# Modulation multiplies gated by weight chunks with tiles loaded two ahead, x_c loaded through ScalarE's queue, and two more raw buffers for the feed-forward output

## The chip, the core and the metric

The kernel runs on one core of a Trainium2 chip. The core's engines work side by side, each through its own instructions in a fixed order: PE (TensorE, matmuls; PEld is its weight load), DVE (VectorE), ACT (ScalarE), POOL (GpSimd) and SP (SyncE, which here only issues DMAs). ACT and POOL issue DMAs too. The metric is the device time of one execution in microseconds (us). Three runs of the kernel before gave 1420.67, 1426.11 and 1424.01, a median of 1424.01.

## What is computed

Two layers over 256 latent and 256 context tokens of width 1024, all in float32. Layer 0 mixes tokens with a bidirectional mLSTM, layer 1 with latent attention; a gated feed-forward with a short convolution follows each. Around every sub-layer stands an adaptive normalization, whose scales, shifts and gates come from a conditioning vector:

```python
m = jax.nn.silu(cond) @ w + b                 # six vectors of 1024 a layer ("modulation")
h = x * (1 + scale) + shift
x = layer_norm(ALPHA * x + gate * sublayer(h))
```

There are two conditionings, c for latent and c_ctx for context tokens. The modulation is a product of a vector with a 1024 x 6144 matrix in each layer. This case is about where that product is done.

## The kernel before

Each float32 matmul is made of three (`mm3`, lines 375 to 377): a weight and an activation are each split into a rounded high part, cast by ACT (L315 for weights, L380 for activations), and a low remainder, subtracted by DVE (L318, L381); then high x high, high x low and low x high are accumulated.

**The weight stream** (`Stream`). Weights come in chunks of 128 x 1024 floats, 512 KB, in one order fixed by `_plan`. SP loads a chunk into a raw buffer (L273), ACT and DVE split it into one of three `w` buffers (NB = 3), PE multiplies. So at most two chunks are split ahead of the one in use. There are three raw buffers of their own; some stages borrow others, as the rings in `Stream.__init__` say: during w_v also `acc`, `ar` and `u` tiles (11 in all), from `("fout0", 0, 0)` the two `acc`, from `("aout", 0, 0)` the three `ar`. A borrowed buffer is free only when its last user has read it.

**The stages**, with the time PE spends on one chunk: a start-up with the first five `up` chunks; `w_up` (5.46 us), which also evacuates x_m and x_c (a convolution of x_m) to DRAM through POOL; `w_og` (5.46), with the background generator `x_sums`, which reads x_m back; `w_v` (2.73), two halves p = 0 and 1 that multiply sums of blocks; `gates`; four heads of `w_qk` (8 chunks of 5.46 each) with the attention of the head before in the background; the output projection `mout`, context then latent (2.73); LayerNorm; feed-forward 0 (`ffn_pre`, `ffn_in`, then `fout0` at 2.73); and layer 1.

**Background work.** `bg` and `bg2` are Python generators; `tick(n, n2)` after a chunk takes n steps of the first and adds n2 to an account that buys steps of the second. This places instructions in the program. Outside the start-up, where the order is written out by hand, the tile library then orders each engine's instructions at build time: of those whose inputs are there by its own estimate, the one earliest in the program comes first. So an instruction without a data dependency can be pulled far ahead of its place. The order is fixed when the kernel runs: an instruction that waits holds all behind it on its engine.

**The modulation in the background** (`bg2`). For each of the vectors (layer l, index c), `ada_bg` takes eight tiles of 128 x 1024 of the transposed matrix. For each tile and condition, one DVE multiply (L506, 128 x 1024) with `bc[j]`, the SiLU of the condition broadcast to all partitions, leaves the sum of its products in one column. There are 80 tiles and 128 multiplies: two a tile for c = 2 to 5 of layer 0 and c = 0, 1 of layer 1, one a tile for the rest. A generator step is one multiply. Vectors 0 and 1 of layer 0 are made in the start-up by PE. The vector (0, 2), a gate, goes with `w_og`; the other nine go with the query-key heads, `mout` and `ffn_in`. A gate's columns are transposed and written to DRAM (L513 to L516).

**The pace.** The tiles of the matrix lie in three `ar` buffers. So that the order does not pull their loads far ahead, `pace` (L518) makes each load wait for the stream: ACT copies one element of the last used weight chunk to `tok` (L521), POOL copies it into the tile (L522), and only then may SP's DMA (L501) write the tile. `bc` is loaded in the same way (L531) and passes through SiLU (L532).

**x_c.** `xc_load` (L682) reads x_c back from DRAM through POOL's queue and splits it. It is called from the second half of `w_v`, after 6 of its first 16 chunks and 10 of its last 12; nothing else holds these loads but a free `s2` buffer.

Of the kernel before, what the change touches and what calls it, by code (L numbers as in the profile page):

```python
# [7 lines left out]
F32 = mybir.dt.float32  # L8
# [20 lines left out]
NEG = -1e30  # L29
CW = 1024  # L30

NB, NRAW, NU, NAR, NS = 3, 3, 31, 3, 15

SUMS = 5

# [3 lines left out]

VE = {1: (3, 0), 2: (3, 0), 3: (3, 0)}  # L40

ADA_T, ADA_Q, ADA_M, ADA_F = 1.25, 1.5, 0.5, 1.2

# [10 lines left out]
TAIL = {"mout": 4, "fout0": 6, "aout": 7, "fout1": 6}  # L54
# [174 lines left out]
class Stream:  # L229


    def __init__(self, k, ids, order, ws):
        self.k, self.ids, self.order, self.ws = k, ids, order, ws
        self.n = len(order)
        self.nl = self.ns = self.nu = 0
        self.live, self.kept = [], []
        self.limit = self.n
        self.raw, self.hl, self.tags = {}, {}, {}
        self.nsum = 0

        keys = [x[0] for x in order]
        self.bufs = [(0, [("raw", NRAW)] * NRAW)]
        self.bufs.append((keys.index(("vt2", 0, 0)), [("acc", 2)] * 2 + [("ar", NAR)] * NAR + [("u", NU)] * 3 + self.bufs[0][1]))
        self.bufs.append((keys.index(("gates", 0, 0)), self.bufs[0][1]))
        self.bufs.append((keys.index(("fout0", 0, 0)), self.bufs[-1][1] + [("acc", 2)] * 2))
        self.bufs.append((keys.index(("aout", 0, 0)), self.bufs[-1][1] + [("ar", NAR)] * NAR))

    def ring(self, j):
        return [x for x in self.bufs if x[0] <= j][-1]
# [97 lines left out]
class K:  # L347
# [141 lines left out]
    def ada_bg(self, l, c, nconds):  # L489


        nc = self.nc
        if c in (2, 5):
            v = self.adav
            col = v[:, 0:8 * nconds].rearrange("p (j k) -> p k j", k=8)
        else:
            col = self.modc[l, c][:, :, 0:nconds]
        for k in range(8):
            w = self.pool.tile([128, 1024], F32, tag="ar", name="ar", bufs=NAR)
            self.pace(w)  # L500
            nc.sync.dma_start(w, self.a["adaT"][l, c, k])  # L501
            for j in range(nconds):
                if j:
                    yield
                o = self.pool.tile([128, 1024], F32, tag="junk", name="junk", bufs=1) if j + 1 < nconds else w
                nc.vector.scalar_tensor_tensor(o, w, 1.0, self.bc[j], op0=ALU.mult, op1=ALU.mult,  # L506
                                               accum_out=col[:, k, j:j + 1])
            yield
        b = self.smc("ada_c")[:, 48 * l + 8 * c:48 * l + 8 * c + 8].unsqueeze(2).to_broadcast([128, 8, nconds])
        nc.vector.scalar_tensor_tensor(col, col, 1.0 if c in (1, 4) else 0.0, b, op0=ALU.add, op1=ALU.add)  # L510
        if c in (2, 5):
            t = self.pool.tile([128, 32], F32, tag="adat", name="adat", bufs=1)
            nc.vector.transpose(t, v)  # L513
            for q in range(4):
                nc.sync.dma_start(self.gd[l, c].rearrange("j (k q i) -> q (j k) i", q=4, i=32)[q, 0:8 * nconds],
                                  t[32 * q:32 * q + 8 * nconds])  # L516

    def pace(self, t):  # L518

        k = self.pool.tile([1, 1], F32, tag="tok", name="tok", bufs=6)  # L520
        self.nc.scalar.copy(k, self.st.last[0:1, 0:1].bitcast(F32))  # L521
        self.nc.gpsimd.tensor_copy(t[0:1, 0:1], k)  # L522

    def ada_all(self, items):

        nc = self.nc
        self.bc = []
        for j in range(2):
            r = self.pool.tile([128, 1024], F32, tag="acc", name="bc", bufs=2)
            self.pace(r)  # L530
            nc.sync.dma_start(r, self.a["crow"][j:j + 1, :].to_broadcast([128, 1024]))  # L531
            nc.scalar.activation(r, r, AF.Silu)  # L532
            self.bc.append(r)
        for l, c in items:
            yield from self.ada_bg(l, c, 2 if l == 0 or c < 2 else 1)
        self.bc = None
# [25 lines left out]
    def start_up(self):  # L562

        nc, st = self.nc, self.st
# [5 lines left out]
        w, ps, raws = [], [], []  # L570
        src = self.a["ada_w"][0]
        self.adaw, self.xT = {}, []
        for op, g in LOADS:
            f0, f1 = GROUPS[g] if op != "r" else (0, 0)
            if op == "a":
                wd = 128 * (f1 - f0)
                nk = 512 // wd
                self.adaw[g] = []
                for k in range(8):
                    if k % nk == 0:  # L580
                        t = self.uf("adaw")
                        self.adaw[g].append(t)
                    ap = bass.AP(tensor=src.tensor, offset=src.offset + k * 128 * 6 * D + f0 * 128,
                                 ap=[[6 * D, 128], [D, 2], [1, wd]])
                    c = k % nk * 2 * wd
                    nc.sync.dma_start(t[:, c:c + 2 * wd].rearrange("p (a b) -> p a b", a=2), ap)
            elif op == "x":
                for i in range(f0, f1):
                    x = self.s2("xT")
                    nc.sync.dma_start(x, self.a["tokT"][i])  # L590
                    self.xT.append(x)
            else:
                n, _ = st.ids["up", g, 0]
                r = self.pool.tile([128, 1024], F32, tag="raw" if g < 3 else "ar", name="raw0",
                                   bufs=NRAW if g < 3 else NAR)
                nc.sync.dma_start(r, st.ws[n])
                raws.append(r)

# [73 lines left out]
    def w_up(self):  # L672
        st = self.st
        for m in range(NUP, 16):
            w = st.use(("up", m, 0))
            ps = self.ps("up")
            for k in range(8):
                c = slice(k * 128, (k + 1) * 128)
                self.mm3(ps, (w[0][:, c], w[1][:, c]), (self.hT[k][:, 0], self.hT[k][:, 1]), k == 0, k == 7)
            self.up_evac(m, ps)  # L680

    def xc_load(self, k):  # L682
        x = self.s2("xcr")
        self.nc.gpsimd.dma_start(x, self.xcd[k])
        u = self.u("xc")
        self.split(u[:, 0], u[:, 1], x)
        self.xc.append(u)
# [573 lines left out]
    def ffn_in(self, l, hT, n, nt, pre=()):  # L1261
        nc, st = self.nc, self.st
        cw, cb = self.smc("fcw%d" % l), self.smc("fcb%d" % l)
        key = "fin%d" % l
        acts = []
        pre = list(pre)
        for p in range(NF):
            pss = []
            for j in range(2):
                if pre:  # L1270
                    w, ps = pre.pop(0)
                    self.ffn_half(ps, w, hT, 1)
                    if not pre:
                        st.unhold()
                else:
                    w = st.use((key, p, j))
                    ps = self.ps("fin")
                    for k in range(8):
                        c = slice(k * 128, (k + 1) * 128)
                        hi, lo = hT(k)  # L1280
                        self.mm3(ps[:, :n], (w[0][:, c], w[1][:, c]), (hi, lo), k == 0, k == 7)
                pss.append(ps)
                self.tick(nt, ADA_F)
            tmp = self.s2("fg")
# [110 lines left out]
    def rope_load(self):  # L1395
        self.ropet = []
        for t in range(2):
            r = self.pool.tile([128, 2, 512], F32, tag="ar", name="rope", bufs=NAR)
            self.nc.sync.dma_start(r, self.a["rope"][:, t * 128:(t + 1) * 128, :].rearrange("a p f -> p a f"))
            self.ropet.append((r[:, 0], r[:, 1]))  # L1400

# [173 lines left out]
def build(tc, off, a, out):  # L1575
    es = ExitStack()
    with es:
        k = K(tc, es, off, a)
        nc = k.nc
# [2 lines left out]
        k.setup()  # L1582
        st.skip(NUP)
        k.start_up()
        k.w_up()
        k.bg2.append(k.ada_all(((0, 2),)))
        k.bg = [k.x_sums()]
        k.w_og()
        while k.bg2:
# [23 lines left out]
        hn = lambda i: (k.hn[i][:, 0], k.hn[i][:, 1])  # L1613
# [13 lines left out]
        gate = k.bcast(k.gd[0, 2][1:2, :], "gate")  # L1627
# [17 lines left out]
        pl = k.acc4()  # L1645
        xr = k.res_load(tokr, 2)
        gate = k.bcast(k.gd[0, 2][0:1, :], "gate")
        k.outmm("mout", range(16 - TAIL["mout"]), hn, pl, 256, 16, 1, n2=ADA_M)
        k.drain()
        k.outmm("mout", range(16 - TAIL["mout"], 16), hn, pl, 256, 16, 1, True)  # L1650
        k.hn = {}
# [14 lines left out]
        gate = k.bcast(k.gd[0, 5][1:2, :], "gate")  # L1666
# [88 lines left out]
```

## Time and profile before

| what | value |
|---|---|
| median of three runs | 1424.01 us |
| the profiled execution, its own time | 1425.35 us |
| its span, first to last instruction | 1423.6 us |
| mean granted clock of TensorE | 0.989 |
| busy ACT / POOL | 690.2 us (48%) / 159.0 us (11%) |
| moved by DMA | 288.97 MB, mean 203 GB/s |
| modulation tiles, issue to landing | 3.3 / 3.6 / 10.6 us (least, median, most) |
| x_c loads, issue to landing | 5.3 / 6.2 / 14.7 us |

The profile is one execution of the kernel, recorded by the chip. An engine's busy time is the time in which it runs instructions, without DMA issues and semaphores. A wait is idle time of an engine ahead of an instruction, put down to the event that ended it ("PE sc L376 <- DVE qk L381" means that PE stood before a matmul of line 376 into the tile `sc`, until DVE's line 381 had written `qk`; then the total, the number and the longest). A timeline gives start, duration, engine, line, operation, tiles, and in brackets the idle time before. An x with a number counts instructions. The granted clock is the share of full speed that TensorE was given. In 20 us windows it is 1.00 from 0 to 420 and then below 0.98 in six places: 0.74 in 420 to 440, 0.95 and 0.96 in 620 to 660, 0.84 in 720 to 740, 0.91 in 1080 to 1100 and in 1220 to 1240, and at the very end.

PE is idle for 45 us of the span: 9.7 in the first 40 us (start-up), 4.1 from 1400 on, 6 in layer 1 and the rest in the stages from `w_v` to the start of feed-forward 0.

### The profile page before, as it was taken

The page shows a single profiled execution, that of the slowest core. Times are in us where ns is not written, and L with a number is a line of the kernel's source. Part 1 is how long each engine was busy: PE and PEld are TensorE (multiplying, and loading weights), DVE is VectorE, ACT ScalarE, POOL GpSimd, SP SyncE. Part 2 cuts the span into 40 slices and gives each one's busy share as a digit, 9 for nine tenths or more (in the row PEclk, how much of TensorE's full clock was granted, in tenths as well). Part 3 has the DMA queues.
Part 4 walks back from the last instruction along what each step waited for, and adds up shares of the span by engine and source line. Part 5 has one row for each costly group of instructions (what it writes and reads, how often), then busy time and mean ns, then how long its engine had stood idle before and what let it go on. Part 6 is the DMA issues. An engine that isn't in the chain of part 4 may idle for free.

```text
span 1423.6 us, 19222 instructions
## 1 busy us (share of the span) xinstructions
PE 1378.8 (97%) x6969; PEld 1159.0 (81%) x6969; DVE 1032.5 (73%) x1627; ACT 690.2 (48%) x1113; POOL 159.0 (11%) x293
## 2 busy tenths in 40 slices
PE   7999999999998999989989999999999999999997
PEld 3788887777777888878888888888888988899986
DVE  6677856687577687878889776764577888867764
ACT  6576443345433355364644343334364667555551
POOL 0023100112111011102012000120000001000000
PEclk9999999999998999999999999999999999999999
DMA  9477867777654454637647566686665424467660
GB/s 339 160 242 272 324 222 249 253 261 212 217 186 163 133 192 132 213 129 280 223 155 260 191 209 209 219 276 215 193 203 189 140 87 164 148 188 224 211 207 30
DMA packets 90238, 288.97 MB, mean 203 GB/s; under 512 B 11288, under 2 KB 19736, under 8 KB 90144
## 3 DMA queue, kind: packets, MB, share of 16 engines
q1 hardware_dynamic: 69824, 224.29, 46.7%
q0 software_dynamic: 16576, 54.56, 11.9%
q10 hardware_dynamic: 3744, 8.91, 1.6%
q8 instruction: 54, 0.88, 0.3%
q14 instruction: 40, 0.33, 0.1%
HBM read 261.46 MB, written 26.26 MB: 202 GB/s over the span
## 4 chain that ended last, share of the span: by engine, by line
PE 76%; DMA 10%; DVE 6%; issue 4%; ACT 2%; POOL 1%; SPq 0%; DVEq 0%; POOLq 0%; ACTq 0%
PE fin L375 8%; PE fin L377 8%; PE fin L376 8%; PE y L376 5%; PE y L377 5%; PE y L375 5%; DMA raw<-in_ws 4%; PE qk L375 3%; PE qk L376 3%; PE qk L377 3%; PE tok L376 3%; PE tok L377 3%; PE tok L375 3%; DMA ar<-in_adaT 2%; PE up L375 2%
## 5 line engine op out<-in xcount | busy, mean ns | idle before, releaser
L315 ACT CAST w<-raw 128x1024 fp32r<-128x1024 f32 (+2 forms) x289 | 301.5, 1045 | 321.5 <-PE fin L377 81.1
L318 DVE TENSOR_TENSOR w<-raw,w 128x1024 fp32r<-128x1024 f32 (+2 forms) x289 | 350.2, 1214 | 138.9 <-ACT w L315 138.2
L375 PE MATMUL fin<-h,w 128*128 128x256 f32 (+1 forms) x696 | 232.1, 335 | 0.0
L376 PE MATMUL fin<-h,w 128*128 128x256 f32 (+1 forms) x696 | 232.1, 334 | 0.0
L377 PE MATMUL fin<-h,w 128*128 128x256 f32 (+1 forms) x696 | 231.8, 334 | 0.0
L375 PEld LDWEIGHTS fin<-h,w 128*128 128x128 f32 x696 | 132.9, 192 | 12.8
L376 PEld LDWEIGHTS fin<-h,w 128*128 128x128 f32 x696 | 132.8, 191 | 12.9
L377 PEld LDWEIGHTS fin<-h,w 128*128 128x128 f32 x696 | 132.7, 191 | 12.7
L506 DVE SCALAR_TENSOR_TENSOR ar<-ar,bc 128x1024 f32<-128x1024 f32 x80 | 97.8, 1222 | 41.5 <-DMA ar<-in_adaT 35.6
L375 PE MATMUL qk<-xc,w 128*128 128x512 f32 x256 | 100.9, 394 | 0.0
L377 PE MATMUL qk<-xc,w 128*128 128x512 f32 x256 | 99.9, 390 | 0.0
L376 PE MATMUL qk<-xc,w 128*128 128x512 f32 x256 | 99.9, 390 | 0.0
L506 DVE SCALAR_TENSOR_TENSOR junk<-ar,bc 128x1024 f32<-128x1024 f32 x48 | 58.6, 1220 | 53.1 <-DMA ar<-in_adaT 53.1
L522 POOL COPY ar<-tok 1x1 f32<-1x1 f32 x80 | 42.0, 529 | 482.4 <-ACT tok L521 338.8
L375 PE MATMUL y<-w,act 128*128 128x512 f32 (+1 forms) x212 | 80.4, 379 | 0.0
L376 PE MATMUL y<-w,act 128*128 128x512 f32 (+1 forms) x212 | 80.1, 378 | 0.0
L377 PE MATMUL y<-w,act 128*128 128x512 f32 (+1 forms) x212 | 80.1, 378 | 0.0
L375 PEld LDWEIGHTS qk<-xc,w 128*128 128x128 f32 x256 | 48.2, 188 | 10.1 <-issue 0.4
L377 PEld LDWEIGHTS qk<-xc,w 128*128 128x128 f32 x256 | 48.1, 188 | 10.0
L376 PEld LDWEIGHTS qk<-xc,w 128*128 128x128 f32 x256 | 48.2, 188 | 9.7
L652 ACT ACTIVATE fg<-fg 128x512 f32<-128x512 f32 (+1 forms) x44 | 23.0, 523 | 68.0 <-DVE fg L650 68.0
L318 DVE TENSOR_TENSOR wu<-raw,wu 128x1024 fp32r<-128x1024 f32 x36 | 43.4, 1221 | 10.5 <-ACT wu L315 9.8
(399 smaller groups left out, 3043.2 us busy)
## 6 DMA issues: line engine op xcount, KB each, us to landing
raw<-in_ws SPq DMA_DIRECT2D x306, 512.0 KB, 4.3
ar<-in_adaT SPq DMA_DIRECT2D x80, 512.0 KB, 3.6
adaw<-in_ada_w SPq DMA_DIRECT2D x32, 256.0 KB, 6.0
xmd<-xr POOLq DMA_DIRECT2D x16, 256.0 KB, 2.9
xcd<-cv POOLq DMA_DIRECT2D x16, 256.0 KB, 2.8
xs<-xmd POOLq DMA_DIRECT2D x16, 256.0 KB, 4.5
od<-o ACTq DMA_DIRECT2D x16, 256.0 KB, 6.1
t2d<-raw ACTq DMA_DIRECT2D x8, 512.0 KB, 3.9
```

Source lines behind the costliest of these rows:

```text
L315: k.nc.scalar.copy(h[:, :cols], src)
L318: k.nc.vector.tensor_sub(l[:, :cols], src, h[:, :cols])
L375: mm(out, w[0], x[0], start=start, stop=False)
L376: mm(out, w[0], x[1], start=False, stop=False)
L377: mm(out, w[1], x[0], start=False, stop=stop)
L506: nc.vector.scalar_tensor_tensor(o, w, 1.0, self.bc[j], op0=ALU.mult, op1=ALU.mult, accum_out=col[:, k, j:j + 1])
L522: self.nc.gpsimd.tensor_copy(t[0:1, 0:1], k)
L652: nc.scalar.activation(tmp[:, :n], tmp[:, :n], AF.Silu)
```

## The change

- **The pace is replaced by a gate.** `pace` is gone. `gate` is one ACT copy of an element of the last used weight chunk, and it goes into the column where the multiply will leave its sum (partition 0). The multiply, not the load, must now wait for that chunk. POOL takes no part.
- **Tiles are loaded two ahead.** `ar_load` takes the next tile of a list; two are loaded when `ada_all` starts, and the first step of each tile loads one more before its multiplies. The three buffers are now tags `ar` (2) and `ar1` (1) in turn.
- **Steps.** A step is one multiply, as before. New are three steps of prologue: after the `bc` loads come two ends of a step, then the SiLU, then one more. The product now goes to `junk` for both conditions.
- **Where the steps go.** (0, 2) starts with `w_up`, one step a chunk, and goes on in `w_og` with 0.8 (1.25 before). The others: 1.6 steps a chunk in the heads (1.5 before), 0.6 in `mout` (0.5), 1.3 in `ffn_in` (1.2) but none at p = 0; and none in the latent `mout` after its sixth chunk (12 before).
- **x_c** is loaded through ACT's queue, each load behind a gate on its own tile.
- **Raw buffers.** `fout0` borrows the two `acc`, `ar1` and `junk`, four instead of two, but from its ninth chunk on; from `aout` on two `ar` are added, nine in all instead of eight.

```diff
-NB, NRAW, NU, NAR, NS = 3, 3, 31, 3, 15
+NB, NRAW, NU, NS = 3, 3, 31, 15
-ADA_T, ADA_Q, ADA_M, ADA_F = 1.25, 1.5, 0.5, 1.2
+ADA_U, ADA_T, ADA_Q, ADA_M, ADA_F = 1, 0.8, 1.6, 0.6, 1.3
@@ Stream.__init__
-        self.bufs.append((keys.index(("vt2", 0, 0)), [("acc", 2)] * 2 + [("ar", NAR)] * NAR + [("u", NU)] * 3 + self.bufs[0][1]))
+        self.bufs.append((keys.index(("vt2", 0, 0)), [("acc", 2)] * 2 + [("ar", 2), ("ar", 2), ("ar1", 1)] + [("u", NU)] * 3 + self.bufs[0][1]))
         self.bufs.append((keys.index(("gates", 0, 0)), self.bufs[0][1]))
-        self.bufs.append((keys.index(("fout0", 0, 0)), self.bufs[-1][1] + [("acc", 2)] * 2))
-        self.bufs.append((keys.index(("aout", 0, 0)), self.bufs[-1][1] + [("ar", NAR)] * NAR))
+        self.bufs.append((keys.index(("fout0", 0, 8)), self.bufs[-1][1] + [("acc", 2)] * 2 + [("ar1", 1), ("junk", 1)]))
+        self.bufs.append((keys.index(("aout", 0, 0)), self.bufs[-1][1] + [("ar", 2)] * 2))
@@ ada_bg
         for k in range(8):
-            w = self.pool.tile([128, 1024], F32, tag="ar", name="ar", bufs=NAR)
-            self.pace(w)
-            nc.sync.dma_start(w, self.a["adaT"][l, c, k])
+            w = self.art.pop(0)
+            self.ar_load()
             for j in range(nconds):
-                if j:
-                    yield
-                o = self.pool.tile([128, 1024], F32, tag="junk", name="junk", bufs=1) if j + 1 < nconds else w
+                o = self.pool.tile([128, 1024], F32, tag="junk", name="junk", bufs=1)
+                self.gate(col[0:1, k, j:j + 1])
                 nc.vector.scalar_tensor_tensor(o, w, 1.0, self.bc[j], op0=ALU.mult, op1=ALU.mult,
                                                accum_out=col[:, k, j:j + 1])
-            yield
+                yield
@@
-    def pace(self, t):
-
-        k = self.pool.tile([1, 1], F32, tag="tok", name="tok", bufs=6)
-        self.nc.scalar.copy(k, self.st.last[0:1, 0:1].bitcast(F32))
-        self.nc.gpsimd.tensor_copy(t[0:1, 0:1], k)
+    def gate(self, ap):
+
+        self.nc.scalar.copy(ap, self.st.last[0:1, 0:1].bitcast(F32))
+
+    def ar_load(self):
+
+        if self.arq:
+            l, c, k = self.arq.pop(0)
+            w = self.pool.tile([128, 1024], F32, tag=("ar", "ar", "ar1")[self.nar % 3], name="ar", bufs=(2, 2, 1)[self.nar % 3])
+            self.nar += 1
+            self.nc.sync.dma_start(w, self.a["adaT"][l, c, k])
+            self.art.append(w)
@@ ada_all
-            self.pace(r)
+            self.gate(r[0:1, 0:1])
             nc.sync.dma_start(r, self.a["crow"][j:j + 1, :].to_broadcast([128, 1024]))
+            self.bc.append(r)
+        self.arq = [(l, c, k) for l, c in items for k in range(8)]
+        self.art, self.nar = [], 0
+        for _ in range(2):
+            self.ar_load()
+        for _ in range(2):
+            yield
+        for r in self.bc:
             nc.scalar.activation(r, r, AF.Silu)
-            self.bc.append(r)
+        yield
@@ w_up
             self.up_evac(m, ps)
+            self.tick(0, ADA_U)
@@ xc_load
-        self.nc.gpsimd.dma_start(x, self.xcd[k])
+        self.gate(x[0:1, 0:1])
+        self.nc.scalar.dma_start(x, self.xcd[k])
@@ ffn_in
-                self.tick(nt, ADA_F)
+                self.tick(nt, ADA_F if p else 0)
@@ build
+        k.bg2.append(k.ada_all(((0, 2),)))
         k.w_up()
-        k.bg2.append(k.ada_all(((0, 2),)))
...
-        k.outmm("mout", range(16 - TAIL["mout"]), hn, pl, 256, 16, 1, n2=ADA_M)
+        k.outmm("mout", range(6), hn, pl, 256, 16, 1, n2=ADA_M)
+        k.outmm("mout", range(6, 16 - TAIL["mout"]), hn, pl, 256, 16, 1)
```

More of the change, by code (lines that the diff above doesn't have):

```diff
@@ L594, in start_up @@
                 r = self.pool.tile([128, 1024], F32, tag="raw" if g < 3 else "ar", name="raw0",
-                                   bufs=NRAW if g < 3 else NAR)
+                                   bufs=NRAW if g < 3 else 2)
                 nc.sync.dma_start(r, st.ws[n])
@@ L1397, in rope_load @@
         for t in range(2):
-            r = self.pool.tile([128, 2, 512], F32, tag="ar", name="rope", bufs=NAR)
+            r = self.pool.tile([128, 2, 512], F32, tag="ar", name="rope", bufs=2)
             self.nc.sync.dma_start(r, self.a["rope"][:, t * 128:(t + 1) * 128, :].rearrange("a p f -> p a f"))
```

## The prediction

> **What bounds the kernel now.** The sum is made against the profiled execution: span 1423.6, its own time 1425.35, 0.1% above the median 1424.01 of the runs shown. First the page's busy times, then PE's waits, the longest first.
>
> ```profile
> PE 1378.8 (97%) x6969; PEld 1159.0 (81%) x6969; DVE 1032.5 (73%) x1627; ACT 690.2 (48%) x1113; POOL 159.0 (11%) x293
> ...
> PE sc L376 <- DVE qk L381: 7.5, 1, 7.5
> ...
> PE tok L376 <- DVE w L318: 6.4, 7, 2.4
> PE zT L1168 <- DVE z L1141: 6.0, 2, 3.5
> PE hnT L1082 <- DVE oh L1076: 2.6, 1, 2.6
> ```
>
> PE is the bound, and no edit removes a matmul. All that can be won is PE's 45 us of idle time (1423.6 - 1378.8) and the slow matmuls behind it. DVE released PE each time, but DVE's timeline shows that it stood itself:
>
> ```profile
> 428.88 1.23 DVE L506 SCALAR_TENSOR_TENSOR junk<-ar,bc 128x1024 f32<-128x1024 f32 x1 [4.57 <-DMA ar<-in_adaT]
> ...
> 634.34 1.23 DVE L506 SCALAR_TENSOR_TENSOR junk<-ar,bc 128x1024 f32<-128x1024 f32 x1 [3.05 <-DMA ar<-in_adaT]
> ...
> 731.23 1.23 DVE L506 SCALAR_TENSOR_TENSOR junk<-ar,bc 128x1024 f32<-128x1024 f32 x1 [1.30 <-DMA ar<-in_adaT]
> ...
> 271.06 1.23 DVE L284 TENSOR_TENSOR raw<-raw 128x1024 f32<-128x1024 f32 x1 [6.01 <-DMA raw<-in_ws]
> ```
>
> A modulation multiply (L506) stands in DVE's fixed order before its tile has landed, and what PE needs stands behind it: the split of head 0's last keys (428.88), the attention rows (634.34), the LayerNorm rows (731.23). The fourth line is another case, a weight that lands late. Where a tile comes from is in the waits of POOL and DVE:
>
> ```profile
> POOL ar L522 <- ACT tok L521: 338.8, 59, 19.4
> ...
> DVE junk L506 <- DMA ar<-in_adaT: 53.1, 23, 5.3
> ...
> DVE ar L506 <- DMA ar<-in_adaT: 35.6, 24, 3.0
> ```
>
> POOL's copy waits for ACT's token, then SP's load starts, then it lands (3.6 median): the load starts only when the multiply's chunk is due, and DVE stands 88.7 us for it in all.
>
> **What goes.** In order of time, from PE's timeline:
> - *w_v begins.* PE waits 0.79 and 1.06 at 212 and 216, for loads into buffers that (0, 2) keeps until 185. Half of its 16 multiplies move into w_up (11 chunks, one step each, 3 of them prologue); the other 8 and the end need 9 steps at 0.8, so the twelfth w_og chunk instead of the fourteenth, 2 x 5.46 earlier, more than both waits: 1.85.
> - *w_v, 273 to 351.* 2.39, 0.39, 0.71, 0.40, 0.66 = 4.55. Five x_c loads leave POOL from 255.8 to 259.2, one takes 14.7 to land, and weights beside them are late. The code calls for x_c only in the second half (from 296), but nothing in the data holds these loads. The gate does.
> - *End of head 0.* 7.47. Then 8 sc, 7 sl and 2 qk matmuls run slow: 1.87 against 0.96, 2.99 against 1.59 (7 x 0.2275), 0.70 against 0.455, 2.55 more.
> - *626 to 642.* 1.07 and 2.65; then 16 transposes in 3.43 against 1.74 (8 take 0.87 elsewhere) and two matmuls 0.40 late: 5.8.
> - *713 to 740.* 0.33 and 3.49. Four multiplies (4 x 1.2) and the 1.30 wait lie among the LayerNorm's instructions, 6.1 in all, more than the 3.49. Now none is emitted from the seventh chunk of the latent mout to p = 0 of the feed-forward. Slow matmuls: 15 transposes 3.11 against 1.63, 3 fin 0.79 against 0.36, 10 fin 2.13 against 1.20, 2.84: 6.7.
>
> Sum 1.85 + 4.55 + 10.0 + 5.8 + 6.7 = **28.9**, the most that goes. With tiles two ahead, a load starts when the tile three back is used up and has two tiles' steps to land: with two multiplies a tile, 4 steps at 1.6 a chunk of 5.46, 13.6 us; with one, 6.8, where landing took 3.6 by the median and 10.6 at worst. Late next: 0.5 at head 0 (the split itself, 0.59 ACT and 0.68 DVE, has 2.5 us of other matmuls beside it, as the trace shows before the stall), 0.5 for a slow landing in mout, 0.5 at the LayerNorm, 2 in w_v, where POOL's accumulating loads still take 8.4 to land. I give back 3.5; bounds 0 and 10.
>
> The slow matmuls are read as a clock that drops: the granted clock is 0.74 from 420 to 440 and 0.84 from 720 to 740. [...]
>
> **What is added.**
> - *DVE: moved, not added.* 128 multiplies of 1.22 before and after, one a step. Heads: 32 ticks x 1.6 = 51 steps less 3 of prologue, 48, as 32 x 1.5 = 48 before. mout: 16 x 0.6 and 6 x 0.6, 13 against 14. ffn_in: the last 51 at 1.3, done in 40 of its 42 ticks. Only w_up gets more, 8 multiplies (9.8) in its last 8 chunks (43.7). There DVE has room:
>
> ```profile
> 70.00:113.00 43.00, 43.00 (x192) 35.61 (x191) 30.84 (x42) 31.43 (x53) 12.06 (x23) 1.00 0.69 238
> ```
>
> Columns: window, length, busy PE, PEld, DVE, ACT, POOL, clock, DMA share, GB/s. DVE 30.84 + 9.8 = 40.6 of 43, and weights are split two chunks (10.9) ahead: 0. Were that cover gone, each multiply in front of a split would cost its 1.22, 9.8. DMA: 12.8 MB in 57 to 113 and some 4.2 (two bc, six tiles), 304 GB/s, where w_og carried 278. I take 0.5.
> - *The gate's wait.* Behind a gated multiply stand DVE's splits, and PE waits for those. But the chunk it waits for was cast about two chunks before its use. In the heads it holds no one longer than ar's DMA did: 0 to 5, I take 1.
> - *ScalarE.* 148 gates for 84 token copies of 0.186 are 12 us more, 16 x_c issues of 0.33 are 5, on an engine that is 48% busy: 0. What an issue holds when its buffer is not free is a rival below.
> - *POOL* loses 80 copies (42 us) and their wait; its loads go earlier. No wait of PE's names them: 0.
> - *SP.* A tile's load waits for the multiplies three tiles back, with weight loads behind it, where it waited for POOL (212.9 us in all) with the same behind it: 0, and up to 3 if a load is held too long.
> - *Raw buffers.* PE has no gap in 740 to 1080, so two more win 0. The first eight fout0 chunks get three instead of five. The mout chunks run at the same pace (2.73) on three, and there the casts wait for PE, not for loads:
>
> ```profile
> ACT w L315 <- PE y L377: 12.8, 9, 1.7
> ACT w L315 <- DMA raw<-in_ws: 3.8, 1, 3.8
> ```
>
> 0; with the heads' landing (6.9) a round of (6.9 + 1.05 + 1.23) / 3 = 3.1 would cost 8 x 0.33 = 3.
>
> [...] No row here separates queue and gate.
>
> **Sum.** 1425.35 - 28.9 + 3.5 + 0.5 + 1 = **1401.5**, forecast 1402.
>
> **The rivals.** 0.5% (7 us) is about what a measurement can tell from no change: 1417 to 1431 is the same.
> - *The forecast*, 63%: from 1396 (all of 28.9) to 1410.
> - *Half the gain*, 14%: x_c is bunched again. Ten loads also left POOL together in the second half, from 338 to 346, when buffers came free. Now all 16 (10 at one a chunk of 2.73) lie beside w_v's heaviest loads, 512 to 1024 KB a chunk. If w_v loses 4.55 again instead of winning it, and the LayerNorm is late by itself (1.95 at 1087 without any multiply, and its slow matmuls, 5 in all): 1402 + 9 + 5 = 1416, just faster.
> - *Waits change places*, 11%: gated multiplies bunch where a chunk is late, and DVE's wait for ar becomes one for the gate. If the three DVE stalls remain (10.0 + 5.8 + 6.7) and w_v's 6.4 less 2 goes: 1425.35 - 4.4 = 1421. For it: 141 waits of DVE for ACT's casts (138.2 us). Against it: a gate is done with the cast, two chunks early.
> - *Slower: ScalarE held by x_c*, 10%. An issue that waits for a free s2 buffer holds the casts behind it, in w_v. A cast has two chunks, 5.46, less its 1.05 and DVE's 1.23: 3.2 of room. A hold as long as an x_c landing (6.2) would cost 16 x 3.0 = 48 and the 4.55: 1402 + 53 = 1455. It is slower than before from holds of (23 - 4.55) / 16 + 3.2 = 4.4. Against it: od and t2d issues already stand in ACT's order, 0.33 each, without such a wait.
> - *The gate doesn't do what it says*, 2%: were dependencies kept by whole tile, copy and multiply would take turns, slower. But PE's L375 starts before L318 has written the other half of the same w.
>
> Faster 0.77, same 0.11, slower 0.12. The range goes from 1395, just under the full gain, to 1422, the third case; the slower ones stay out.
>
> **What would show it.** PE's waits for qk L381 and oh L1076 gone, for z L1141 under 3; DVE's waits for ar under 25 instead of 88.7; DVE's busy time in the heads unchanged; x_c issues at even steps after 296; no clock under 0.9 between 400 and 800. Wrong: casts that stand behind an x_c issue, weights late in w_v, or DVE waiting for gates.

## The result and the profile after

The changed kernel took **1404.93 us** (median of 4 runs, 1402.88 to 1405.57), the kernel before 1424.66 (4 runs, 1420.67 to 1426.11): a ratio of 0.9863, 95% interval 0.9841 to 0.9886. The forecast was 1402, its range 1395 to 1422. The profiled execution took 1404.94, its span is 1403.2 us and its mean granted clock 0.997 (0.989 before).

First the busy times of the changed kernel's page, then PE's waits, the longest first, as for the kernel before.

```profile
PE 1371.7 (98%) x6969; PEld 1152.3 (82%) x6969; DVE 1029.9 (73%) x1627; ACT 696.0 (50%) x1177; POOL 107.4 (8%) x193
```

```profile
PE adar L466 <- ACT adas L380: 6.6, 1, 6.6
PE tok L376 <- DVE w L318: 6.2, 6, 2.6
PE adar L466 <- DVE adas L381: 2.0, 3, 0.8
PE zT L1183 <- DVE z L1156: 1.8, 1, 1.8
```

The first and third lines belong to the start-up, and the last `zT` line to layer 1. PE's idle time fell from 44.8 to 31.5 us (1403.2 - 1371.7), and its busy time by 7.1 with the same 6969 matmuls: those are the slow matmuls that are gone. The waits for `qk` (7.5) and `oh` (2.6) have left the list, the one for `z` fell from 6.0 to 1.8: its 3.49 at the LayerNorm is gone, and what is left stands at 1204 in layer 1 (2.55 there before). The one for `tok`, in `w_v`, stands at 6.2 as before (6.4).

Why the first three went is in the answer for the tile `ar`: what DVE's multiplies waited for, and, last, how long the tiles took to land.

```profile
L504 DVE SCALAR_TENSOR_TENSOR junk<-ar,bc x128: 1191/1217/1229, 82.4 to 924.3; 128x1024 f32<-128x1024 f32 x128
...
  ACT bc L545: 3.4, 1
  ACT mod L518: 0.8, 1
...
DMA to landing us min/median/max: 3.8/4.5/5.8
```

The same 128 multiplies now wait once for SiLU (3.4) and once for a gate (0.8), never for a tile; before, tiles held DVE for 88.7 us. They land no faster (4.5 by the median, 3.6 before). They are simply there when the multiply's turn comes.

Where the time went, stage by stage. A stage runs from its first matmul to that of the next; each row is one profiled execution, in us.

| kernel | start | w_og | w_v | gates, head 0's keys | heads | mout | ffn 0 in | fout0 | dkv | rest | span |
|---|---|---|---|---|---|---|---|---|---|---|---|
| before | 121.1 | 87.0 | 161.4 | 52.6 | 190.5 | 109.5 | 248.6 | 116.9 | 37.0 | 299.0 | 1423.6 |
| after | 122.6 | 87.1 | 162.2 | 52.5 | 180.3 | 106.5 | 242.7 | 114.2 | 36.1 | 299.0 | 1403.2 |
| after, a second execution | 120.7 | 87.0 | 160.9 | 52.6 | 180.3 | 106.0 | 242.7 | 114.2 | 36.1 | 298.2 | 1398.7 |

The end of head 0 gave 10.2, `mout` 3.0, the LayerNorm at the head of feed-forward 0 5.9, and `fout0` with `dkv` 3.6, which was not forecast. `w_v` gave nothing. The start-up and `w_v` differ by 1 to 2 us between two executions of one program (the second one here is that of e12 below), so differences of that size in them are read from waits, not from lengths.

### The profile page after: what moved, and what is told of

It is laid out like the page before. It is cut to its first block, busy times and chain, and to the rows that moved or that the text cites. A ratio compares the mean times of both kernels' runs of the same rounds, so it can differ in the third digit from the quotient of the medians.

```text
span 1403.2 us, 19109 instructions
## 1 busy us (share of the span) xinstructions
PE 1371.7 (98%) x6969; PEld 1152.3 (82%) x6969; DVE 1029.9 (73%) x1627; ACT 696.0 (50%) x1177; POOL 107.4 (8%) x193
## 4 chain that ended last, share of the span: by engine, by line
PE 86%; DMA 6%; DVE 5%; ACT 2%; issue 1%; SPq 0%; DVEq 0%; ACTq 0%
PE fin L376 9%; PE fin L375 9%; PE fin L377 9%; PE y L376 6%; PE y L377 6%; PE y L375 5%; PE qk L375 4%; PE qk L377 4%; PE qk L376 4%; PE tok L376 4%; PE tok L377 4%; PE tok L375 4%; DMA raw<-in_ws 3%; DMA xcr<-xcd 2%; PE up L375 2%; PE up L377 2%
## 5 line engine op out<-in xcount | busy, mean ns | idle before, releaser
L318 DVE TENSOR_TENSOR w<-raw,w 128x1024 fp32r<-128x1024 f32 (+2 forms) x289 | 350.2, 1214 | 178.2 <-ACT w L315 177.8
L315 ACT CAST w<-raw 128x1024 fp32r<-128x1024 f32 (+2 forms) x289 | 301.8, 1046 | 322.5 <-PE fin L377 106.8
L504 DVE SCALAR_TENSOR_TENSOR junk<-ar,bc 128x1024 f32<-128x1024 f32 x128 | 155.8, 1217 | 5.5 <-ACT bc L545 3.4
L375 PEld LDWEIGHTS qk<-xc,w 128*128 128x128 f32 x256 | 48.1, 188 | 10.1 <-issue 0.4
L318 DVE TENSOR_TENSOR wu<-raw,wu 128x1024 fp32r<-128x1024 f32 x36 | 43.5, 1220 | 13.0 <-ACT wu L315 12.4
L375 PE MATMUL up<-hT,w 128*128 128x512 f32 x128 | 50.5, 394 | 0.5 <-ACT hT L380 0.5
L376 PE MATMUL up<-hT,w 128*128 128x512 f32 x128 | 50.1, 392 | 0.4 <-DVE hT L381 0.4
```

What stands on the lines that cost most here:

```text
L315: k.nc.scalar.copy(h[:, :cols], src)
L318: k.nc.vector.tensor_sub(l[:, :cols], src, h[:, :cols])
L375: mm(out, w[0], x[0], start=start, stop=False)
L376: mm(out, w[0], x[1], start=False, stop=False)
```

## The experiments

Their stages, as in the table above:

| kernel | w_v | heads | mout | ffn 0 in | fout0 | dkv | median us | ratio to before, interval |
|---|---|---|---|---|---|---|---|---|
| e1, gate and lead alone | 163.6 | 180.3 | 108.3 | 242.7 | 117.2 | 35.4 | 1405.65 | 0.987 (0.9852 to 0.9888) |
| e2, x_c through POOL again | 163.8 | 180.3 | 106.8 | 242.7 | 114.2 | 36.1 | 1404.46 | 0.9855 (0.9839 to 0.9871) |
| e3, x_c split two calls later | 162.5 | 180.2 | 105.8 | 242.6 | 114.2 | 36.1 | 1403.50 | 0.9851 (0.9832 to 0.9869) |
| e4, raw buffers as before | 160.1 | 180.3 | 107.6 | 242.7 | 116.7 | 35.4 | 1405.04 | 0.9866 (0.9844 to 0.9888) |
| e5, loads held, multiplies free | 161.3 | 182.0 | 108.7 | 248.6 | 114.4 | 36.1 | 1413.49 | 0.9933 (0.991 to 0.9955) |
| e6, no lead in the program | 163.1 | 180.2 | 106.3 | 242.7 | 114.2 | 36.1 | 1403.36 | 0.9864 (0.9841 to 0.9887) |
| e7, no x_c loads | 155.0 | 180.2 | 106.5 | 242.7 | 114.2 | 36.1 | 1396.42 | 0.9818 (0.9794 to 0.9842) |
| e8, no stored sums | 155.3 | 180.3 | 105.6 | 242.7 | 114.2 | 36.1 | 1395.56 | 0.9811 (0.9782 to 0.9839) |
| e9, first three tiles gated | 158.8 | 180.3 | 105.7 | 242.7 | 114.1 | 36.2 | 1402.12 | 0.9843 (0.982 to 0.9866) |
| e10, x_c earlier | 165.8 | 180.2 | 106.0 | 242.7 | 114.2 | 36.1 | 1407.51 | 0.9874 (0.9854 to 0.9894) |
| e11, e9 and e10 together | 168.6 | 180.3 | 106.0 | 242.7 | 114.3 | 36.1 | 1408.78 | 0.9886 (0.9867 to 0.9904) |
| e12, the changed kernel again | 160.9 | 180.3 | 106.0 | 242.7 | 114.2 | 36.1 | 1402.86 | 0.9852 (0.9828 to 0.9877) |

The stages are those of one execution of each kernel, the times medians of all. For e1 and e2 the execution shown is their slowest (1409.13 and 1407.07), for e9, e10 and e12 their fastest (1399.51, 1405.31, 1400.51). e9 to e12 ran on one chip, beside 1425.53 of the kernel before.

### What made the heads and the LayerNorm faster: e1, e5, e6

**e1** keeps the gate and the two-ahead list and takes the rest back: x_c through POOL, the old raw buffers, all of (0, 2) in `w_og` (at 1.6 a chunk), and the old rates and places in the heads, `mout` and `ffn_in`.

```diff
-ADA_U, ADA_T, ADA_Q, ADA_M, ADA_F = 1, 0.8, 1.6, 0.6, 1.3
+ADA_U, ADA_T, ADA_Q, ADA_M, ADA_F = 0, 1.6, 1.5, 0.5, 1.2
-                self.tick(nt, ADA_F if p else 0)
+                self.tick(nt, ADA_F)
-        k.outmm("mout", range(6), hn, pl, 256, 16, 1, n2=ADA_M)
-        k.outmm("mout", range(6, 16 - TAIL["mout"]), hn, pl, 256, 16, 1)
+        k.outmm("mout", range(16 - TAIL["mout"]), hn, pl, 256, 16, 1, n2=ADA_M)
```

> Only the gate and the two-ahead loading are in; x_c, the raw buffers and the places of the steps are as before, except that (0, 2) goes with w_og at 1.6 steps a chunk, since its three prologue steps must fit before w_v. Theory (the gain is DVE no longer standing for tiles): the heads lose about 10 us, mout 3, the start of feed-forward 0 about 4 of its 5.9, since the multiplies still stand among the LayerNorm's instructions but do not wait; w_v 0 to 2: 1405 to 1409. Rival (the places matter, not the lead): the heads keep most of their 7.5 us stall and feed-forward 0 all of its 3.5: 1415 or more.

Measured: 1405.65, heads 180.3 and feed-forward 242.7, both as in the changed kernel. So the new pace alone carries those 16 us, and moving the multiplies out of the LayerNorm's stretch adds nothing to it: four multiplies of 1.2 stand among the LayerNorm's rows in e1 as before, and PE does not wait for them. The expectation missed `mout`, which won 1.2 instead of 3, and `w_v`, which lost 2.2. Against the changed kernel, e1 lacks 1.8 in `mout`, 1.4 in `w_v` and 2.3 in `fout0` with `dkv`.

**e5** swaps what is held: each load waits again for ACT's token and POOL's copy, two tiles ahead in the program, and the multiplies have no gate.

```diff
-                self.gate(col[0:1, k, j:j + 1])
...
+    def pace(self, t):
+        k = self.pool.tile([1, 1], F32, tag="tok", name="tok", bufs=6)
+        self.nc.scalar.copy(k, self.st.last[0:1, 0:1].bitcast(F32))
+        self.nc.gpsimd.tensor_copy(t[0:1, 0:1], k)
...
+            self.pace(w)
             nc.sync.dma_start(w, self.a["adaT"][l, c, k])
```

> The changed kernel with the old release: each tile's load, still asked for two tiles ahead, waits for ACT's token and POOL's copy, and the multiplies are not gated. Theory (the lead is what counts: a tile that has two tiles' steps to land is there, however it is released): heads within 2 us of 180.3 and feed-forward 0 within 1 of 242.7, DVE's waits for ar under 25 us, 1403 to 1408. Rival (the gate counts: as long as the load is what is released, the order pulls the multiply to where the load ends by its estimate, and DVE stands for late landings): heads 185 or more, waits for ar 40 or more, 1412 or more.

Measured: 1413.49, and the feed-forward is back at 248.6. DVE's waits in e5, then PE's, and last DVE and PE at the LayerNorm:

```profile
DVE junk L503 <- DMA ar<-in_adaT: 81.7, 36, 8.4
```

```profile
PE zT L1188 <- DVE z L1161: 7.2, 3, 4.1
...
PE sc L376 <- DVE qk L381: 1.5, 1, 1.5
```

```profile
719.62 1.23 DVE L503 SCALAR_TENSOR_TENSOR junk<-ar,bc 128x1024 f32<-128x1024 f32 x1 [4.28 <-DMA ar<-in_adaT]
...
726.58 3.46 PE L1188 MATMUL zT<-ident,z 128*128 128x128 f32 x15 [4.10 <-DVE z L1161]
```

Two tiles of lead in the program do not help while the load is what waits: DVE stands 81.7 us for tiles (88.7 before), 4.28 of them among the LayerNorm's rows, and PE waits 4.10 behind it (3.49 before). The rival forecast this, but was wrong on the heads: at head 0 only 1.5 of the 7.5 came back, so they take 182.0 and not 185. The multiply ahead of the split stood 0.93 us there, for 4.57 before. The price of a late tile depends on what stands behind its multiply.

**e6** keeps the gate and gives up the lead: a tile's load is written just before its own multiplies.

```diff
-            w = self.art.pop(0)
             self.ar_load()
+            w = self.art.pop(0)
...
-        for _ in range(2):
-            self.ar_load()
```

> The changed kernel without the lead: each tile is asked for in the first step of its own, the gates stay. Theory (lead in the program): the loads start late and DVE stands for them again, heads 185 or more, 1411 or more. Rival (nothing but a free buffer holds a load any more, so the order pulls it ahead by itself and the written lead adds nothing): heads 180 to 181, 1403 to 1406.

Measured: 1403.36 and heads of 180.2, no difference, as the rival said. The loads left SP just as early relative to the stream; SP in the changed kernel and in e6, at one place of head 0 (e6 lies 1.2 us earlier as a whole):

```profile
428.12 0.33 SPq L526 DMA_DIRECT2D ar<-in_adaT  x1
```

```profile
426.95 0.33 SPq L526 DMA_DIRECT2D ar<-in_adaT  x1
```

With nothing but a free buffer to hold it, the library pulls the load ahead by itself. So of "steps released by chunks, tiles two ahead" the first half is the mechanism; the second is what three buffers give anyway.

### The raw buffers: e4

```diff
-        self.bufs.append((keys.index(("fout0", 0, 8)), self.bufs[-1][1] + [("acc", 2)] * 2 + [("ar1", 1), ("junk", 1)]))
-        self.bufs.append((keys.index(("aout", 0, 0)), self.bufs[-1][1] + [("ar", 2)] * 2))
+        self.bufs.append((keys.index(("fout0", 0, 0)), self.bufs[-1][1] + [("acc", 2)] * 2))
+        self.bufs.append((keys.index(("aout", 0, 0)), self.bufs[-1][1] + [("ar", 2), ("ar", 2), ("ar1", 1)]))
```

> The changed kernel with the old raw buffers of fout0 (five from the first chunk) and eight from aout on. Theory (the two more buffers remove the 1.95 us stall before ckT and its slow matmuls): fout0 up to ckT takes 116.9 instead of 114.2, dkv to dq 37.0 instead of 36.1, 1408 to 1409. Rival (the stall went because the stage runs at another moment, or with the modulation): 1405, stages as in the changed kernel.

Measured: the total, 1405.04, can't tell it from 1404.93, but the stage can: `fout0` and `dkv` take 152.1 together, against 150.3 after and 153.9 before. At the end of `fout0`, DVE in the kernel before, in e4 and in the changed kernel (each from its last weights to `ckr`):

```profile
1082.61 3.50 DVE L318 TENSOR_TENSOR wu<-raw,wu 128x1024 fp32r<-128x1024 f32 x3 [3.31 <-ACT wu L315]
...
1087.06 0.48 DVE L1300 TENSOR_SCALAR ckr<-dkv,rs 128x256 f32<-128x256 f32 x1
```

```profile
1064.01 3.50 DVE L318 TENSOR_TENSOR wu<-raw,wu 128x1024 fp32r<-128x1024 f32 x3 [2.64 <-ACT wu L315]
...
1068.46 0.48 DVE L1315 TENSOR_SCALAR ckr<-dkv,rs 128x256 f32<-128x256 f32 x1
```

```profile
1062.12 1.22 DVE L318 TENSOR_TENSOR wu<-raw,wu 128x1024 fp32r<-128x1024 f32 x1 [0.94 <-ACT wu L315]
1065.24 1.23 DVE L318 TENSOR_TENSOR wu<-raw,wu 128x1024 fp32r<-128x1024 f32 x1 [1.90 <-ACT wu L315]
...
1067.58 0.48 DVE L1315 TENSOR_SCALAR ckr<-dkv,rs 128x256 f32<-128x256 f32 x1
```

With the old buffers the last three `wu` chunks land late and are split in one block ahead of `ckr`, for which PE stands 1.95 (before) or 1.79 (e4); with two more buffers the block is broken up and PE has no wait there. e1, with the old buffers, has it too (2.2). The theory is right in the wait, and in `fout0` (116.9 expected, 116.7 measured); its `dkv` of 37.0 did not come (35.4), since no slow matmuls follow the wait in e4. So the buffers are worth 1.8 by e4. The 3.6 from before to after are this wait and, in the kernel before, the slow matmuls behind it.

### Why w_v gained nothing: e2, e3, e7 to e11

PE's waits in `w_v`, first the kernel before, then the changed kernel, where the stage lies 1.6 us later:

```profile
273.48 0.50 PE L376 MATMUL tok<-w,xm 128*128 128x512 f32 x1 [2.39 <-DVE w L318]
...
296.92 0.50 PE L376 MATMUL tok<-w,s 128*128 128x512 f32 x1 [0.71 <-DVE w L318]
```

```profile
294.24 0.50 PE L376 MATMUL tok<-w,s 128*128 128x512 f32 x1 [2.55 <-DVE w L318]
...
332.87 0.49 PE L375 MATMUL tok<-w,x 128*128 128x512 f32 x1 [1.26 <-ACT w L315]
334.13 0.50 PE L376 MATMUL tok<-w,x 128*128 128x512 f32 x1 [0.77 <-DVE w L318]
343.56 0.50 PE L376 MATMUL tok<-w,s 128*128 128x512 f32 x1 [0.98 <-DVE w L318]
```

With the small ones they come to 6.40 before and 7.45 after (5.76 in the second execution). The waits at 212 and 216 (1.85) did go, and so did those at 273 and 277 (2.39 and 0.39). But the late weight of 297 stands at 294 now with 2.55, while x_c's first load, held by its gate as meant, left ACT only at 298.8; and behind 310 there are waits of 4.53, for 0.66 before. ACT in the changed kernel, ahead of two of them:

```profile
309.93 0.33 ACTq L699 DMA_DIRECT2D xcr<-xcd  x1
...
317.58 0.62 ACT L380 CAST xc<-xcr 128x512 fp32r<-128x512 f32 x1 [5.18 <-DMA xcr<-xcd]
318.11 1.05 ACT L315 CAST w<-raw 128x1024 fp32r<-128x1024 f32 x1
...
331.25 0.62 ACT L380 CAST xc<-xcr 128x512 fp32r<-128x512 f32 x1 [4.76 <-DMA xcr<-xcd]
331.78 1.04 ACT L315 CAST w<-raw 128x1024 fp32r<-128x1024 f32 x1
```

Each x_c load is issued and its cast waits for it in ACT's order: 24.7 us over 12 waits. The weight cast at 331.78 is the one that PE waits for at 332.87. In the chain of work that ended last, x_c's landings take 29.9 of the 50 us from 300 to 350. That gave a first theory, the held casts: ACT held by x_c keeps weights from being cast. **e2** undoes the queue and the gate, **e3** keeps them and moves each split two calls behind its load.

```diff
-        self.gate(x[0:1, 0:1])
-        self.nc.scalar.dma_start(x, self.xcd[k])
+        self.nc.gpsimd.dma_start(x, self.xcd[k])
```

> The changed kernel with x_c on POOL's queue and ungated, as before. Theory (the gated x_c costs w_v, since its casts stand in ScalarE's order and wait for their landing in front of weight casts): w_v 2 to 4 us shorter than the 162.2 of the changed kernel, 1401 to 1403. Rival (the gate spares w_v the bunched loads, as the prediction had it): w_v longer by about 4.5, 1409.

```diff
+            self.xq.append(x)
+        if self.xq and (len(self.xq) > 2 or self.nxc == 16):
+            x = self.xq.pop(0)
             u = self.u("xc")
             self.split(u[:, 0], u[:, 1], x)
```

> The changed kernel with x_c split two calls after its load is issued; queue, gate and number of loads are unchanged. Theory (casts wait for landings of about 6 us, and weight casts behind them): ACT's 25 us of waits for x_c fall under 5, w_v 3 to 5 us shorter, 1400 to 1402. Rival (the DMA engines are short in that half, whoever issues and whenever it is cast): w_v within 1 us of 162.2, 1405.

Measured: `w_v` 163.8 and 162.5, against 162.2 and 160.9 of the changed kernel; totals 1404.46 and 1403.50. Neither edit moves the stage by more than it varies, so none of the lengths forecast by the theories came (e3's rival, within 1 us, was met). The waits inside the stage say more. In e2 ACT stands only 7.0 us for x_c, and PE's waits behind 310 are 2.46, for 4.53; but the late weight of 273 is back. In e2, DVE's sum of weights that waits for it and PE's row; then the same sum in the changed kernel:

```profile
270.43 1.23 DVE L284 TENSOR_TENSOR raw<-raw 128x1024 f32<-128x1024 f32 x1 [5.72 <-DMA raw<-in_ws]
...
272.84 0.50 PE L376 MATMUL tok<-w,xm 128*128 128x512 f32 x1 [2.09 <-DVE w L318]
```

```profile
266.48 1.23 DVE L284 TENSOR_TENSOR raw<-raw 128x1024 f32<-128x1024 f32 x1 [2.62 <-DMA raw<-in_ws]
```

The three kernels without the gate have this wait (2.39 before, 2.11 in e1, 2.09 in e2); none with the gate has it. So at 273 the prediction was right: bunched x_c loads made that weight late, and holding them ended it (the gate and ACT's queue together; no run separates the two). e3 did not bring about what it was to test, since ACT still stands 22.5 us for x_c, 8.32 of them at once:

```profile
319.52 0.62 ACT L380 CAST xc<-xcr 128x512 fp32r<-128x512 f32 x1 [8.32 <-DMA xcr<-xcd]
320.04 1.04 ACT L315 CAST w<-raw 128x1024 fp32r<-128x1024 f32 x1
...
321.13 0.79 PE L375 MATMUL tok<-w,x 128*128 128x512 f32 x1 [3.94 <-ACT w L315]
```

So e3 does not refute the held casts; its rows show one. The weights of these casts had landed long before: those cast at 318.11 and 331.78 in the changed kernel are of the first loop, and DVE's last sum of that loop's weights, which reads them, ran at 309.73. The waits at 320.47, 332.87 and 334.13, 0.76 + 1.26 + 0.77 = 2.8, are the held casts' in the changed kernel (2.9 in the second execution). No run takes the casts out of ACT's order and leaves the loads, so this is read from the rows alone. The other theory was that the stage is short of DMA. **e7** leaves x_c's loads out (POOL fills the tile with 0.5), **e8** leaves out the detour of `w_v`'s block sums through DRAM (the second half then takes those weights without the stored sum).

```diff
-        self.gate(x[0:1, 0:1])
-        self.nc.scalar.dma_start(x, self.xcd[k])
+        self.nc.gpsimd.memset(x, 0.5)
```

> The changed kernel with the 16 x_c loads left out: POOL sets the tile to a constant instead, so queries, keys and gates are computed from it. Theory (w_v is slow since x_c's 4 MB share its DMA time and ACT's casts wait for them): w_v 154 to 157 instead of 162.2. Rival (w_v's own weights are late, with or without x_c): 159 to 162.

```diff
-        if key[0] == "vt4":
-            k.nc.sync.dma_start(t, k.t2d[key[1]][key[2]])
-            k.nc.gpsimd.dma_start(t, self.ws[n], accum_op=ALU.add)
-        elif key[0] != "vt2":
+        if key[0] != "vt2":
...
-            if key[0] == "vt2":
-                k.nc.scalar.dma_start(k.t2d[key[1]][key[2]], src)
```

> The changed kernel in which vt4 is loaded plainly from the weights: the stored sum is neither written nor read back, and POOL's accumulating load is left out, so vt4's product uses the wrong weight. Theory (x_c makes w_v slow): w_v stays within 2 us of 162.2. Rival (the detour through DRAM, 4 times 512 KB a half each way, and the accumulating loads of 7 to 9 us are what makes weights late): 153 to 157.

Measured: 155.0 and 155.3, 6 to 7 us less by either (against 160.9 and 162.2). PE's waits for `w_v`'s weights in e7:

```profile
PE tok L376 <- DVE w L318: 2.1, 2, 1.7
```

These two, 1.70 at 291.9 and 0.39, are the late weight of 294 again, without any x_c load. All later waits of PE in this stage are gone with x_c's 4 MB, and all but one of 0.54 with e8's 8 MB of stores and loads. Both kernels take bytes away at different places and win about the same. That fits a shortage of DMA, and it fits the held casts as well: with x_c's loads gone nothing holds ACT, and with the detour gone ACT stands 15.6 us for x_c instead of 24.7 (and DVE 10.1 for x_c's casts instead of 16.2). As I read these rows, the two are not rivals: where the DMA engines are fuller (1.00 and 0.90 busy from 310 to 320 and from 320 to 330 in the changed kernel, 0.68 and 0.69 in e8) ACT stands longer for x_c, and its order passes that on to weights that have long landed. Whether the queue that issues x_c matters was not shown: e2 changes queue and gate together (163.8 against 162.2).

Next, which part of the stage is short? I took the second loop of the second half for the crowded one and moved x_c out of it: **e9** gates the first three modulation tiles, so that their loads leave with the heads (SP had issued them from 343.5 to 346.7); **e10** calls for x_c after 12 chunks of the first loop and 4 of the second; **e11** does both.

```diff
+            if self.nar < 3 and (l, c) != (0, 2):
+                self.gate(w[0:1, 0:1])
```

```diff
-                    if p == 1 and i and name in ("v11", "vt1"):
+                    if p == 1 and i:
```

> The changed kernel, but the loads of the first three tiles of the nine later vectors wait behind an ACT copy each from the last used weight chunk, so that they leave with the heads' chunks; in the changed kernel SP issued three of them from 343.5 to 346.7, in the second half of w_v. Theory (w_v, 162.2 us here, is short of DMA, and every MB that leaves its crowded second half shortens it): 1.5 MB of the 19.2 MB moved in 296 to 373, about 6 us at 249 GB/s, of which the part beside PE's last waits counts: w_v 159 to 161, total 1402 to 1403. Rival (these loads stand behind the weights in SP's order and take nothing from them): w_v 162, total 1405.

> The changed kernel, but x_c is called after each of the last 12 of the first loop's chunks of w_v's second half and after 4 of the second loop's, instead of 6 and 10; the second loop has the heavier other loads. Theory (short of DMA where it is crowded): demand is evened out, PE's waits for weights in w_v fall from 7.5 to 4 or less, w_v 158 to 160, total 1401 to 1402. Rival (what counts is the sum of w_v's loads, as leaving 4 MB out gained 7 wherever they were): w_v 162, total 1404 to 1405.

> The two edits before together. Theory (crowding): w_v 157 to 159, total 1399 to 1401, the floor being the 155 of the kernels without x_c's loads or without the stored sums. Rival (the sum of the loads): w_v 160 to 162, since 1.5 MB do leave w_v, total 1403 to 1405.

> The changed kernel itself, beside the three on the same chip, since what tells them apart is 2 to 5 us. Both theories: 1403 to 1406, w_v 162 within the 1.5 that this stage has varied between executions.

Measured: e9 1402.12 beside 1402.86 of e12, no difference that can be told. e10 and e11 are 5 and 6 us slower by their medians; their intervals touch that of e12, but their `w_v`, 165.8 and 168.6, lies outside the 158.8 to 163.8 of all kernels that load the same bytes. The theory as I put it fell. The busy times by 10 us, for e12 and then e10 (from the left: window, length, five engines, clock, DMA share, GB/s):

```profile
300.00:310.00 10.00, 10.00 (x45) 8.28 (x45) 9.27 (x9) 4.88 (x7) 0.90 (x1) 1.00 0.89 267
310.00:320.00 10.00, 9.12 (x39) 7.00 (x38) 3.19 (x4) 2.98 (x5) 1.15 (x2) 1.00 0.89 326
320.00:330.00 10.00, 8.63 (x38) 6.55 (x36) 4.26 (x5) 4.40 (x7) 0.60 (x1) 1.00 0.94 237
...
350.00:360.00 10.00, 9.23 (x40) 7.25 (x39) 7.85 (x9) 7.45 (x15) 0.00 (x0) 1.00 0.38 120
```

```profile
310.00:320.00 10.00, 7.59 (x33) 5.72 (x32) 5.70 (x6) 4.18 (x7) 0.88 (x1) 1.00 0.99 331
320.00:330.00 10.00, 9.07 (x38) 6.63 (x36) 3.75 (x4) 2.70 (x7) 0.86 (x1) 1.00 1.00 261
330.00:340.00 10.00, 7.74 (x26) 6.00 (x27) 6.97 (x9) 7.40 (x13) 0.03 (x1) 0.83 0.69 219
```

From 300 to 330 the DMA engines are busy 0.89 to 0.94 in the changed kernel; the second loop has room at its end (0.38 from 350). e10 put x_c where the DMA was almost full already: 0.99 and 1.00, PE idle 2.4 of 10 us, and a clock of 0.83 behind it. Here too ACT stands for x_c (5.71 until 314.68), and PE waits 1.66 and 0.76 for the weight cast behind it. A full share alone is not a wait: in e7 it is 0.88, 0.81 and 0.97 in the same three windows, and PE has none. So more of x_c in the first loop costs, and its casts in ACT's order are where. Whether fewer than the present six calls in that loop would gain was not tried, nor a cast of x_c that no weight stands behind. Of the kernels that leave nothing out, none is measurably faster than the changed kernel.

## Why the prediction was right, point by point

The time was 2.9 over the forecast. Several terms were not what made it so.

- **What bounds the kernel: right.** PE idle, DVE standing before a tile not yet landed. With that wait gone (88.7 to nothing), PE's waits behind it went.
- **End of head 0: right.** 10.0 less 0.5 forecast, 10.2 measured, slow matmuls included.
- **LayerNorm at 713 to 740: right in size, half right in cause.** 6.7 less 0.5 forecast, 5.9 measured. The prediction gave two causes, late tiles and the place of four multiplies; e1 wins it all with the places as before, and e5, with a late tile, loses it. But the late tile is not all. The last rows were ready 12.4 us after the stage's first matmul before and 8.5 in e1, and PE gets there at 8.9. Of these 3.9, the tile's wait is 1.3; a weight split with its wait, 1.7, no longer stands among the rows in the newly built order, and they start 0.7 earlier.
- **626 to 642: too large.** 5.8 less 0.5 forecast, 3.0 measured, 3.5 in the second execution. The 2.65 and the slow transposes behind it went (16 take 2.06 now, for 3.43). The 1.07 did not, and was counted in error: it is no late multiply's, PE stands 1.06 for a weight at 618.20, 13.5 us into the stage as before, and so in e1 (1.07) and e5 (1.08). PE also has 0.26, 0.20 and 0.76 for other weights (0.33 before). Kernels with the same `mout` vary from 105.6 to 107.6, so the rest stays open.
- **w_v: the step that failed**, where the prediction takes all 4.55 from 273 to 351 for weights late beside bunched x_c loads and lets the gate win them but for 2. 1.85 and 4.55 less 2, and 0.5 for DMA, make a gain of 3.9; measured are a loss of 0.8 and, in the second execution, a gain of 0.5. The gate held x_c as forecast (issues from 298.8 to 362.2), and 1.85 and the 2.8 at 273 went. But the weight that is late at 294 is so without any x_c load (e7, 1.70), and behind 310 came 4.5 instead of 0.7, 2.8 of it for weights whose cast stands behind an x_c that lands late. The rival "half the gain" was right that x_c lies beside the stage's heavy loads now; its loss of 4.55 and its late LayerNorm did not come. The rival "ScalarE held by x_c" had the engine right and the reason wrong: not an issue without a buffer holds the casts but a landing, and it costs some 3 us, not 48.
- **The gate's wait: right.** 1 forecast, 0 to 5 its bounds; DVE waited 0.8 us once. DVE's waits for ACT's weight casts rose from 138.2 to 177.8, but the time does not go with them: e5 has 141.0 and is slower than the changed kernel, e1 has 191.6 and is not measurably so.
- **Raw buffers: wrong**, 0 forecast with a loss of up to 3 as its bound; 3.6 gained in the stages, of which e4 shows 1.8 to be the buffers' own. The step looked for PE's gaps from 740 to 1080 and found none; the gap that these buffers close lies at 1087, beyond the window that was looked at. The prediction even named that wait (1.95) in another place, as a LayerNorm matter.
- **POOL, SP and ScalarE's gates and issues: right at 0.** An x_c issue takes 0.33 in the changed kernel and never stood for a buffer. What ScalarE's order costs is in the point on `w_v`.

The total came close in part by luck, since what failed was made up elsewhere. Against the terms, the profiled execution lost 4.7 in `w_v`, 2.3 in `mout`, 1.5 in the start-up (which varies) and 0.3 at the LayerNorm; it won 3.6 at `fout0`, 0.7 in the heads and the 1 set aside for the gate: 3.5 in all, the distance from 1401.5 to 1404.94. Sign and size came from the three DVE stalls, 19.1 of the 20.4 us.

Of what the text said would show it, all came: the waits named, DVE's waits for tiles under 25, DVE's busy time in the heads (140.4 before, 139.4 after), x_c's issues, and a granted clock of 1.00 from 400 to 800. Two marks for "wrong" came as well, in `w_v` alone: casts that stand behind x_c (24.7), and weights late there.

## What to carry to other kernels

Where background work shares an engine that runs in a fixed order, let the loads run as far ahead as buffers allow and hold the consumer: in e5 the held loads left DVE standing 81.7 us for tiles, with all that was queued behind it, while the held multiplies of the changed kernel stood 0.8 us for a gate. x_c is the counter-case here: the gate holds its load, and its cast, for which ACT stands 24.7 us, passes the landing on to the weight casts behind it (2.8 us of PE's waits). Before moving loads within a stage, look at the DMA share in slices of 10 us, and at what stands behind the instruction that waits for the landing. And look for a changed buffer's effect in all of the stage that uses it, up to the first instruction queued behind its last chunk.

## What was not expected of the hardware

Here the granted clock did not follow the length of an idle time alone. PE stood 2.55 at 294 in the changed kernel, and its next matmuls ran at full pace, 0.23 apart (granted clock 1.00 from 290 to 300). In e3 it stood 3.94 at 321, and the next ones were slow at once, 0.43 apart. It stood 1.95 at 1087 in the kernel before, and here the slow ones began 1.1 us later (0.88 from 1086 to 1100):

```profile
1087.60 0.44 PE L1348 MATMUL ckT<-ident,ckr 128*128 128x128 f32 x2 [1.95 <-DVE ckr L1300]
...
1088.34 0.67 PE L1348 MATMUL ckT<-ident,ckr 128*128 128x128 f32 x4
1088.69 0.75 PE L375 MATMUL y<-wu,act 128*128 128x512 f32 x1
1089.24 0.63 PE L376 MATMUL y<-wu,act 128*128 128x512 f32 x1
...
1091.80 0.56 PE L376 MATMUL y<-wu,act 128*128 128x512 f32 x1
1092.20 0.39 PE L377 MATMUL y<-wu,act 128*128 128x512 f32 x1
```

They lie 0.43 apart until 1091.8, some 3.5 us in all. After 1.79 at the same place in e4 the matmuls ran at full pace, 0.23 apart (1.00 from 1063 to 1080). Two of the stalls that the prediction counted are of the slow kind too: in the kernel before, `sl` matmuls lay 0.43 apart behind the 7.47 at 431, for 0.23, and a transpose took 0.214 behind the 2.65 at 638, for 0.109. So 1.95 and 2.65 were followed by slow matmuls, and 1.79 and 2.55 were not. What decides was not shown by any run.
